# Value products in groups of four key blocks, the transposed maxima three half key blocks later, and three feature chunks around the change of token halves

## Chip, cores and metric

The kernel runs on one core of a Trainium2 chip. The metric is device time in microseconds of one execution, as the median of several runs.

## What is computed

A decoder block over 2048 tokens of width 1024. One input projection of the normalised tokens feeds two branches. Branch A is latent attention with 8 heads, dense and causal. Branch B is sparse attention with 8 query heads and 2 key/value heads: an indexer scores every visible key, and each query keeps its 256 best.

```python
rel = jax.nn.relu(jnp.einsum('bqhd,bsd->bqhs', qib, k_idx))     # indexer, 8 heads
score = jnp.einsum('bqhs,bqh->bqs', rel, wb)                    # then causal mask
_, sel = lax.top_k(score, k_top)                                # k_top = 256
...
merged = sigmoid(m_a + b_merge[0]) * (o_a @ w_branch_mla) + sigmoid(m_b + b_merge[1]) * (o_b @ w_branch_dsa)
x = x + merged @ w_out
```

`o_a` and `o_b` are the softmax attentions of the two branches, each times the SiLU of its own gate projection.

## The kernel before

The work goes in four stages. **Tokens** (0 to about 344 us of the span): normalise, transpose, project queries, keys and index inputs. The transposed tokens are kept as a high and a low part, `hT0h`, `hT0l`, `hT1h`, `hT1l`, each 128 partitions by 8 by 512 floats (2 MiB), and only 1024 of the 2048 tokens fit; the first half goes to DRAM as `d_h` while the second half is projected.

**Features** (344 to about 1083 us): 96 feature chunks, 24 column groups (gates and merge gates) by 4 groups of 512 tokens. `FEATURES` is their order: first the token half that is on the chip, column group by column group, on `hT0` and then `hT1`; then the other half, which `load_h(g)` brings back from `d_h` into the same two tile pairs as soon as the last chunk that reads them is through. Around that change of halves the order takes two column groups on `hT0` and then the same two on `hT1`, so that a reload has two chunks of time. `load_w` and `load_split` bring the weights of a column group into three buffers `wf`. Each chunk is 24 matmuls in four slots. Between the slots, three lanes are advanced at fixed rates: `index_pair` (the indexer's scores of two query tiles into a tile `sc`, two buffers), `search` (a threshold search on the scores of the pair before: five rounds of a ScalarE Sign pass over each of the two tiles, then mask, removal and bias; 1.3 of its pieces a slot), and `prepare` (queries and keys of branch A).

**Attention** (1058 to 1967 us): `pipeline` runs 32 units (branch, group of 512 queries, pair of heads), of 4, 8, 12 or 16 key blocks. A key block is, for each of two heads, the scores `st` (L646, for branch B with eight small mask products more), Exp on ScalarE into `pt` (L674) and the row sums `acc` (L684, one head on GpSimd, one on VectorE). The value products `o` (L690) are held back: `flush` lets them go in groups of two key blocks, by the first half of a later key block. They use 64 columns of the array for each head, all the other products here use 128. Between the halves `fill` takes pieces of the coming units at an even rate: each piece is one product `ap` (L600) whose row maximum VectorE reads (L604 or L607); then a piece with the last reductions and `nm` (L614); then the piece that transposes the 8 columns of maxima on TensorE (L623), copies them (L625) and sends them by DMA into a row of the coming unit's query tile. `LEAD` is how many half key blocks ahead of the unit's start the pieces are to be through. `finish` multiplies `o` by the gates `og` (L700), stores it, and for every second unit sums the `acc` tiles over the partitions (L708).

**Merge** (1967 to 2339 us): branch projections, merge, output projection.

TensorE's order is the order in which the program is written. The order on the other engines and on the DMA queue is set by a planner at build time, which takes what is ready in its own model of time and prefers what is written earlier.

Of the kernel before, what the change touches and what calls it, by code (L numbers as in the profile page):

```python
# [20 lines left out]
P = 128  # L21
# [19 lines left out]
PREPARE_GAP = 17  # L41
SEARCH_RATE = 1.3
PRIORITY = 200
SEARCH_GAP = 4
INDEX_FIRST = 7
HEADS_FIRST = 10
TAIL = 3
WAIT = 0
LEAD = 6
PT_BUFS = 10  # L50
WINDOW = 8.5
EVALS = 5
PAIRS = [(NT - 1 - n, 2 + n) for n in range(7)]
# [18 lines left out]
class Block:  # L72
# [133 lines left out]
    def hidden(self, tok, t):  # L206
        nc = self.nc
        x = tok.tile([P, D], F32, name="x", tag="x", bufs=X_BUFS)
        nc.sync.dma_start(x, self.a["x"][t * P:(t + 1) * P, :])
        if t == 0:  # L210
            nc.sync.dma_start(self.gnorm, bcast(self.a["norm_gain"], D))
        junk = tok.tile([P, D], BF, name="xj", tag="xj")
        ssq = tok.tile([P, 1], F32, name="xs", tag="xs", bufs=2)
        nc.scalar.activation(junk, x, AF.Square, accum_out=ssq)
        rstd = self.rsqrt(tok, ssq, 1, 1.0 / D, "x")
        nc.vector.scalar_tensor_tensor(x, x, rstd, self.gnorm, op0=OP.mult, op1=OP.mult)
        yield
        i, sl = t % 8, slice(t % 4 * P, t % 4 * P + P)
        hi, lo = (m[:, :, sl] for m in self.hT[i // 4])
        for b in range(2):  # L220
            ps = self.pp.tile([P, 4, P], F32, name="tr", tag="tr", bufs=3)
            for k in range(4):
                kc = 4 * b + k
                nc.tensor.transpose(ps[:, k], x[:, kc * P:(kc + 1) * P], self.ident)
            self.split(nc.scalar, hi[:, 4 * b:4 * b + 4], lo[:, 4 * b:4 * b + 4], ps, eng_lo=nc.vector)
        if t < 8:
            for s, m in enumerate((hi, lo)):
                self.move(self.d_h[t][:, s], m)

    def load_w(self, pool, src, n, name, bufs, engines, stage=None):  # L230
        nc = self.nc
# [101 lines left out]


    def load_h(self, g):
        for i in range(4):
            for s in range(2):
                self.move(self.hT[g][s][:, :, i * P:(i + 1) * P], self.d_h[4 * g + i][:, s])

    def feat(self, ev, hf, g, c, w):  # L340
        nc = self.nc
# [63 lines left out]
    def search(self, ip, n, ts, scs):  # L405
# [27 lines left out]
        for e in range(EVALS):  # L433
# [3 lines left out]
            for i, sc in enumerate(scs):  # L437
                W = sc.shape[1]
                nc.scalar.activation(junk(W), sc, AF.Sign, bias=nt[:, i], accum_out=sg[:, i])  # L439
            v.scalar_tensor_tensor(d, sg, 0.5, guess[:, :, 1:2], op0=OP.mult, op1=OP.add)  # L440
            ma = ip.tile([P, 2, 2, 1], I32, name="ma", tag="ma", bufs=2)
            v.tensor_scalar(ma[:, :, 0], d, 0.0, None, op0=OP.is_gt)
# [14 lines left out]
        for i, (t, sc) in enumerate(zip(ts, scs)):  # L457
# [6 lines left out]
            for r in range(2):  # L464
                v8 = ip.tile([P, 8], F32, name="v8", tag="v8", bufs=2)
                pen = ip.tile([P, 8], F32, name="pen", tag="pen", bufs=2)
                need = ip.tile([P, 1], F32, name="need", tag="need", bufs=2)
                v.max(v8, sc)
                v.tensor_scalar(need, th[:, i, 1:2], -1.0, float(TOPK - 8 * r), op0=OP.mult, op1=OP.add)
                v.tensor_scalar(pen, self.iota8, need, 3.0e38, op0=OP.is_ge, op1=OP.mult)  # L470
                v.tensor_tensor(v8, v8, pen, op=OP.add)
                yield
                v.match_replace(sc, v8, sc, SELECTED)
                yield
            bias = ip.tile([P, S], BF, name="bias", tag="bias", bufs=1)[:, :W]
            nc.scalar.activation(bias, sc, AF.Relu, bias=self.shift)
# [216 lines left out]
    def finish(self, u):  # L693
        nc, at = self.nc, self.at
        b, p, g = u["branch"], u["p"], u["g"]
        while any(s[0] is a for s in self.sums for a in u["acc"]):
            self.add_up()
        og = at.tile([P, 512], F32, name="og", tag="og", bufs=2)
        nc.sync.dma_start(og, self.d_f[4 * b + p][g])
        nc.vector.tensor_tensor(og, u["o"], og, op=OP.mult)  # L700
        nc.sync.dma_start(self.d_o[b][g][:, p], og)
# [25 lines left out]
    def pipeline(self, units, ahead):  # L727
        count = len(units)
        heads, spec, left = [None] * count, [None] * count, [0] * count
        begun, born, clock = 0, [0] * count, [0]  # L730

        def begin(n):
            nonlocal begun
            while begun < count and begun - ahead[begun] <= n:
                m = begun
                heads[m] = units[m]()
                spec[m] = next(heads[m])
                left[m] = 8 * (spec[m]["g"] + 1) + 2
                born[m] = clock[0]
                begun += 1  # L740

        def take(n):
            left[n] -= 1
            next(heads[n])

        begin(-1)
# [5 lines left out]

        def flush(keep=1):
            nonlocal after
            if keep and len(values) < 3:
                return
            while len(values) > keep:
                f, u, j = values.pop(0)
# [8 lines left out]
        for n in range(count):  # L767
# [3 lines left out]
            for j in range(u["nk"]):  # L771

                def fill(half):
                    slots, pieces, rate = 2 * (u["nk"] - j) - half - LEAD, 0, 0.0
                    for m in range(n + 1, begun):
                        pieces += left[m]
                        rate = max(rate, pieces / max(slots, 1))
                        slots += 2 * spec[m]["nk"]
                    credit[0] += rate
                    for m in range(n + 1, begun):  # L780
                        while left[m] and credit[0] >= 1.0 and clock[0] >= born[m] + WAIT:
                            take(m)
                            credit[0] -= 1.0

                clock[0] += 1
                values.append((self.scores_t(u, j, fill, flush), u, j))
            after.append((AGE, self.finish, u))
            while n + 1 < count and left[n + 1]:
# [172 lines left out]
    def run(self):  # L961
        nc, a = self.nc, self.a
        self.setup()
        self.d_h = [self.dram([P, 2, KC, P], F32, "d_h%d" % t) for t in range(NT // 2)]
        self.d_qi = [self.dram([P, H, 32], F32, "d_qi%d" % t) for t in range(NT)]
        self.d_c = [self.dram([P, 2, 3, P], F32, "d_c%d" % t) for t in range(NT)]
        self.d_qb = [self.dram([P, H, P], F32, "d_qb%d" % t) for t in range(NT)]
# [244 lines left out]
def feature_order():  # L1212
    order = []
    for half in range(2):
        pairs = [(c,) for c in range(24)]
        pairs = pairs[:22] + [(22, 23)] if half == 0 else [(0, 1)] + pairs[2:]
        order += [(half, g, 24 * half + c) for p in pairs for g in range(2) for c in p]
    return order

# [72 lines left out]
```

## Time and profile before

| | |
|---|---|
| runs | median 2342.23 us (2340.57 to 2347.39, 3 runs) |
| profiled execution | 2340.68 us, span 2338.9 us |
| TensorE matmuls | 2250.8 us busy (96%) |
| VectorE, GpSimd, ScalarE | 1417.3 (61%), 1193.1 (51%), 986.6 us (42%) |
| granted TensorE clock, mean | 0.987 |
| DMA | 326.12 MB, mean 139 GB/s |
| chain that ended last | TensorE 76%, VectorE 9%, GpSimd 6% |

Busy time of TensorE counts each matmul with its modelled end, so consecutive matmuls overlap, and a gap shows only where the pipeline ran empty. The span runs from the first to the last instruction; the time of the execution has 1.8 us around it.

### The profile page before, as it was taken

Reading aid. Unit: us, or ns where it says so; the run is one execution under the profiler, and the core shown is the slowest. Engines: PE = TensorE matmul, PEld = TensorE weight load, DVE = VectorE, ACT = ScalarE, POOL = GpSimd, SP = SyncE. Lnnn points to the kernel's source line nnn. Section 1 sums busy time; section 2 is a strip of 40 time slices with the busy share of each in tenths; the row PEclk is TensorE's granted clock in tenths of the full one; section 3 lists DMA queues with packets and bytes.
Section 4 is the critical chain, followed back from the end, with each engine's and each line's share of the span. In section 5 each row is a group of like instructions: output and inputs, shape, how many; then the busy total and the mean of one; then the engine's idle time right before and its main releaser. Section 6 shows DMA issues by size and latency. Waiting matters only on the chain.

```text
span 2338.9 us, 37920 instructions
## 1 busy us (share of the span) xinstructions
PE 2250.8 (96%) x12882; PEld 1745.5 (75%) x12882; DVE 1417.3 (61%) x3296; ACT 986.6 (42%) x1986; POOL 1193.1 (51%) x1541
## 2 busy tenths in 40 slices
PE   6999999999988999999999999999999999899999
PEld 6999988877776887886555655655655557899988
DVE  6453525588785877856676676677778874322221
ACT  5342325667666677642334434434433443101110
POOL 5875968866754434312344434434774546634432
PEclk9999999999999999999999999999999999999999
DMA  9441345666668655568433322212222102544442
GB/s 311 139 147 54 120 157 166 227 216 196 223 204 262 206 174 180 182 204 240 135 114 102 117 74 64 65 47 71 79 84 82 51 10 78 172 136 141 138 131 77
DMA packets 298100, 326.12 MB, mean 139 GB/s; under 512 B 23408, under 2 KB 228592, under 8 KB 297776
## 3 DMA queue, kind: packets, MB, share of 16 engines
q1 hardware_dynamic: 297392, 323.56, 44.0%
q8 instruction: 101, 1.65, 0.3%
q14 instruction: 95, 0.78, 0.1%
q10 hardware_dynamic: 512, 0.13, 0.0%
HBM read 184.20 MB, written 139.26 MB: 138 GB/s over the span
## 4 chain that ended last, share of the span: by engine, by line
PE 76%; DVE 9%; POOL 6%; issue 3%; ACT 3%; DMA 2%; SPq 0%; DVEq 0%; ACTq 0%; POOLq 0%
PE st L646 18%; PE o L690 11%; PE acc L113 8%; PE acc L115 8%; PE acc L114 8%; PE ap L600 5%; PE ou L115 2%; PE ou L114 2%; PE ou L113 2%; PE br L114 2%; PE br L113 2%; PE br L115 2%; DVE sc L392 2%; PE z L387 2%; ACT junk L439 1%
## 5 line engine op out<-in xcount | busy, mean ns | idle before, releaser
L674 ACT ACTIVATE pt<-st 128x512 f32<-128x512 f32 (+3 forms) x640 | 340.1, 534 | 466.7 <-PE st L646 417.1
L684 POOL TENSOR_TENSOR acc<-acc,pt 128x512 f32<-128x512 f32 (+3 forms) x288 | 328.2, 1140 | 347.8 <-ACT pt L674 337.9
L392 DVE SCALAR_TENSOR_TENSOR sc<-zr,w_i,sc 128x512 f32<-128x512 f32 (+3 forms) x266 | 214.8, 810 | 111.0 <-ACT zr L389 106.9
L646 PE MATMUL st<-Q,K 96*128 96x512 f32 (+3 forms) x960 | 265.8, 384 | 0.6 <-issue 0.6
L604 DVE TENSOR_REDUCE mx<-ap 128x1 f32<-128x512 f32 (+2 forms) x320 | 185.1, 604 | 110.3 <-PE ap L600 63.6
L684 DVE TENSOR_TENSOR acc<-acc,pt 128x512 f32<-128x512 f32 (+3 forms) x288 | 223.4, 776 | 46.5 <-ACT pt L674 43.1
L607 DVE CUSTOM_DVE_ANT_0 mj<-ap,mask 128x512 bf16<-128x512 f32 (+2 forms) x320 | 193.5, 605 | 91.1 <-PE ap L600 81.9
L646 PEld LDWEIGHTS st<-Q,K 96*128 96x128 f32 (+1 forms) x960 | 163.4, 192 | 73.7 <-issue 50.9
L389 ACT ACTIVATE zr<-z 128x512 f32<-128x512 f32 (+3 forms) x304 | 163.0, 545 | 97.1 <-PE z L387 91.5
L113 PE MATMUL acc<-hT1h,wfh 128*128 128x512 f32 x384 | 156.9, 409 | 9.4 <-DMA hT1h<-d_h 7.0
L113 PE MATMUL acc<-hT0h,wfh 128*128 128x512 f32 x384 | 155.2, 404 | 0.7 <-DMA hT0h<-d_h 0.7
L114 PE MATMUL acc<-hT1l,wfh 128*128 128x512 f32 x384 | 151.9, 396 | 1.6 <-DMA d_f<-ev 1.6
L115 PE MATMUL acc<-hT1h,wfl 128*128 128x512 f32 x384 | 152.5, 397 | 0.0
L114 PE MATMUL acc<-hT0l,wfh 128*128 128x512 f32 x384 | 150.9, 393 | 1.1 <-DMA hT0l<-d_h 1.1
L115 PE MATMUL acc<-hT0h,wfl 128*128 128x512 f32 x384 | 151.6, 395 | 0.0
L690 PE MATMUL o<-pt,Vb 128*64 128x512 f32 (+3 forms) x640 | 138.7, 555 | 0.0
L690 PE MATMUL o<-pt,V 128*64 128x512 f32 (+3 forms) x640 | 136.2, 547 | 0.0
L646 PE MATMUL st<-Q,Kd 128*128 128x512 f32 (+3 forms) x320 | 132.9, 416 | 0.0
L106 ACT ACTIVATE mh<-sg 128x256 fp32r<-128x256 f32 x64 | 26.7, 417 | 231.3 <-POOL sg L931 231.2
L929 DVE TENSOR_TENSOR sg<-br,sg 128x256 f32<-128x256 f32 x128 | 53.7, 424 | 115.7 <-PE br L115 102.6
L387 PE MATMUL z<-kT,iqT 128*128 128x512 f32 (+3 forms) x304 | 111.5, 371 | 11.1 <-ACT zr L389 11.1
L646 PE MATMUL st<-Q,Kl 65*128 65x512 f32 (+3 forms) x320 | 117.3, 367 | 0.0
(283 smaller groups left out, 5923.3 us busy)
## 6 DMA issues: line engine op xcount, KB each, us to landing
d_f<-ev SPq DMA_DIRECT2D x96, 256.0 KB
sg<-d_f SPq DMA_DIRECT2D x128, 128.0 KB
wst<-in_w_f SPq DMA_DIRECT2D x96, 128.0 KB
d_w<-wfh SPq DMA_DIRECT2D x24, 512.0 KB
d_w<-wfl SPq DMA_DIRECT2D x24, 512.0 KB
d_q<-phl SPq DMA_DIRECT2D x32, 384.0 KB
d_k<-phl SPq DMA_DIRECT2D x32, 384.0 KB
wfh<-d_w SPq DMA_DIRECT2D x24, 512.0 KB
```

What stands on the lines that cost most here:

```text
L113: mm(ps, lhi, rhi, start=start, stop=False)
L114: mm(ps, lhi, rlo, start=False, stop=False)
L115: mm(ps, llo, rhi, start=False, stop=stop)
L387: nc.tensor.matmul(z[:, :n], qT[:, h], self.kT[:, k0:k0 + n], start=True, stop=True)
L389: nc.scalar.activation(r[:, :n], z[:, :n], AF.Relu)
L392: nc.vector.scalar_tensor_tensor(sc[:, k0:k0 + n], r[:, :n], ws, sc[:, k0:k0 + n], op0=OP.mult, op1=OP.add)
L604: nc.vector.tensor_reduce(mx[:, b:b + 1], ps[:, :n], axis=AX, op=OP.max)
L607: nc.vector.tensor_tensor_reduce(out=junk[:, :n], in0=ps[:, :n], in1=mask[i][:, 512 * b:512 * b + n], scale=1.0, scalar=-3.0e38, op0=OP.su ...
L646: nc.tensor.matmul(banks[hh][:, cols], l, r, start=start and n == 0, stop=stop and n == len(seq) - 1)
L674: nc.scalar.activation(pt[:, n0:], ps[:, n0:], AF.Exp, scale=u["scale"])
L684: eng.tensor_tensor(acc[:, n0:], acc[:, n0:], pt[:, n0:], op=OP.add)
L690: self.nc.tensor.matmul(u["o"][64 * hh:64 * hh + 64, n0:], u["v"](hh, j), pts[hh][:, n0:], start=(j == 0), stop=(j == u["nk"] - 1))
```

## The change

- `GROUP = 4`: value products go in groups of four key blocks; `pt` has 12 buffers for 10, `og` one for two.
- `SETTLE = 3`: the last piece of a unit's maxima, the transposition, is taken only when three half key blocks have passed since the piece before it. `LEAD` is 7 for 6. `WAIT` was 0 and held nothing back.
- The search has a piece boundary behind each Sign pass, one more wait in each of the five rounds, and three more pieces between the last removal and the bias pass of each tile: 53 pieces for 32.
- Around the change of halves the order takes three column groups on `hT0`, then the same three on `hT1`. `d_h` is one DRAM tile for each 512 tokens, and `load_h` fetches it by pairs of the 8 planes, in the order in which the matmuls read them: pieces of 4096 bytes, where it was 512.

```diff
--- before.py
+++ after.py
@@ -41,13 +41,14 @@
 PREPARE_GAP = 17
 SEARCH_RATE = 1.3
 PRIORITY = 200
-SEARCH_GAP = 4
+SEARCH_GAP = 5
 INDEX_FIRST = 7
 HEADS_FIRST = 10
 TAIL = 3
-WAIT = 0
-LEAD = 6
-PT_BUFS = 10
+LEAD = 7
+SETTLE = 3
+PT_BUFS = 12
+GROUP = 4
 WINDOW = 8.5
 EVALS = 5
 PAIRS = [(NT - 1 - n, 2 + n) for n in range(7)]
@@ -225,7 +226,7 @@
             self.split(nc.scalar, hi[:, 4 * b:4 * b + 4], lo[:, 4 * b:4 * b + 4], ps, eng_lo=nc.vector)
         if t < 8:
             for s, m in enumerate((hi, lo)):
-                self.move(self.d_h[t][:, s], m)
+                self.move(self.d_h[t // 4][:, s, :, sl], m)
 
     def load_w(self, pool, src, n, name, bufs, engines, stage=None):
         nc = self.nc
@@ -333,9 +334,9 @@
 
 
     def load_h(self, g):
-        for i in range(4):
+        for k in range(0, KC, 2):
             for s in range(2):
-                self.move(self.hT[g][s][:, :, i * P:(i + 1) * P], self.d_h[4 * g + i][:, s])
+                self.move(self.hT[g][s][:, k:k + 2], self.d_h[g][:, s, k:k + 2])
 
     def feat(self, ev, hf, g, c, w):
         nc = self.nc
@@ -437,6 +438,7 @@
             for i, sc in enumerate(scs):
                 W = sc.shape[1]
                 nc.scalar.activation(junk(W), sc, AF.Sign, bias=nt[:, i], accum_out=sg[:, i])
+                yield
             v.scalar_tensor_tensor(d, sg, 0.5, guess[:, :, 1:2], op0=OP.mult, op1=OP.add)
             ma = ip.tile([P, 2, 2, 1], I32, name="ma", tag="ma", bufs=2)
             v.tensor_scalar(ma[:, :, 0], d, 0.0, None, op0=OP.is_gt)
@@ -471,6 +473,8 @@
                 v.tensor_tensor(v8, v8, pen, op=OP.add)
                 yield
                 v.match_replace(sc, v8, sc, SELECTED)
+                yield
+            for _ in range(3):
                 yield
             bias = ip.tile([P, S], BF, name="bias", tag="bias", bufs=1)[:, :W]
             nc.scalar.activation(bias, sc, AF.Relu, bias=self.shift)
@@ -695,7 +699,7 @@
         b, p, g = u["branch"], u["p"], u["g"]
         while any(s[0] is a for s in self.sums for a in u["acc"]):
             self.add_up()
-        og = at.tile([P, 512], F32, name="og", tag="og", bufs=2)
+        og = at.tile([P, 512], F32, name="og", tag="og", bufs=1)
         nc.sync.dma_start(og, self.d_f[4 * b + p][g])
         nc.vector.tensor_tensor(og, u["o"], og, op=OP.mult)
         nc.sync.dma_start(self.d_o[b][g][:, p], og)
@@ -727,7 +731,8 @@
     def pipeline(self, units, ahead):
         count = len(units)
         heads, spec, left = [None] * count, [None] * count, [0] * count
-        begun, born, clock = 0, [0] * count, [0]
+        begun = 0
+        turn, taken = [0], [0] * count
 
         def begin(n):
             nonlocal begun
@@ -736,11 +741,11 @@
                 heads[m] = units[m]()
                 spec[m] = next(heads[m])
                 left[m] = 8 * (spec[m]["g"] + 1) + 2
-                born[m] = clock[0]
                 begun += 1
 
         def take(n):
             left[n] -= 1
+            taken[n] = turn[0]
             next(heads[n])
 
         begin(-1)
@@ -752,7 +757,7 @@
 
         def flush(keep=1):
             nonlocal after
-            if keep and len(values) < 3:
+            if keep and len(values) <= GROUP:
                 return
             while len(values) > keep:
                 f, u, j = values.pop(0)
@@ -777,12 +782,12 @@
                         rate = max(rate, pieces / max(slots, 1))
                         slots += 2 * spec[m]["nk"]
                     credit[0] += rate
+                    turn[0] += 1
                     for m in range(n + 1, begun):
-                        while left[m] and credit[0] >= 1.0 and clock[0] >= born[m] + WAIT:
+                        while left[m] and credit[0] >= 1.0 and (left[m] > 1 or turn[0] >= taken[m] + SETTLE):
                             take(m)
                             credit[0] -= 1.0
 
-                clock[0] += 1
                 values.append((self.scores_t(u, j, fill, flush), u, j))
             after.append((AGE, self.finish, u))
             while n + 1 < count and left[n + 1]:
@@ -961,7 +966,7 @@
     def run(self):
         nc, a = self.nc, self.a
         self.setup()
-        self.d_h = [self.dram([P, 2, KC, P], F32, "d_h%d" % t) for t in range(NT // 2)]
+        self.d_h = [self.dram([P, 2, KC, 512], F32, "d_h%d" % g) for g in range(2)]
         self.d_qi = [self.dram([P, H, 32], F32, "d_qi%d" % t) for t in range(NT)]
         self.d_c = [self.dram([P, 2, 3, P], F32, "d_c%d" % t) for t in range(NT)]
         self.d_qb = [self.dram([P, H, P], F32, "d_qb%d" % t) for t in range(NT)]
@@ -1213,7 +1218,7 @@
     order = []
     for half in range(2):
         pairs = [(c,) for c in range(24)]
-        pairs = pairs[:22] + [(22, 23)] if half == 0 else [(0, 1)] + pairs[2:]
+        pairs = pairs[:21] + [(21, 22, 23)] if half == 0 else [(0, 1, 2)] + pairs[3:]
         order += [(half, g, 24 * half + c) for p in pairs for g in range(2) for c in p]
     return order
 
```

## Rows read from the trace of the kernel before

**Rows 1.** Windows of attention: us, busy (instructions) of PE PEld DVE ACT POOL, clock, DMA.

```profile
1090.00:1967.00 877.00, 858.40 (x4951) 517.44 (x4949) 625.66 (x1681) 354.12 (x682) 417.47 (x395) 0.99 0.27 79
...
1540.00:1760.00 220.00, 213.75 (x1247) 130.46 (x1247) 170.49 (x467) 87.34 (x167) 123.33 (x116) 0.98 0.23 71
```

**Rows 2.** Waits of TensorE: for whom, us in total, times, longest.

```profile
PE ap L623 <- DVE nm L614: 16.4, 17, 2.2
...
PE z L387 <- ACT zr L389: 11.1, 6, 3.3
...
PE acc L113 <- DMA hT1h<-d_h: 7.0, 1, 7.0
...
PE ap L600 <- DVE mx L607: 1.0, 2, 0.8
```

**Rows 3.** TensorE in time order, a group of value products, branch A: start, us.

```profile
1640.65 0.40 PE L600 MATMUL ap<-Kd,Q 128*128 128x512 f32 x1
1640.89 0.40 PE L646 MATMUL st<-Q,K 97*128 97x512 f32 x1
1641.22 0.65 PE L690 MATMUL o<-pt,V 128*64 128x512 f32 x2
1641.70 1.46 PE L690 MATMUL o<-pt,V 128*64 128x512 f32 x6
1642.13 1.03 PE L690 MATMUL o<-pt,V 128*64 128x512 f32 x4
1643.09 0.73 PE L646 MATMUL st<-Q,K 96*128 96x512 f32 x2
1643.65 0.40 PE L600 MATMUL ap<-Kd,Q 128*128 128x512 f32 x1
```

**Rows 4.** The same in branch B, without and with value products behind the masks.

```profile
1943.60 0.62 PE L646 MATMUL st<-negb,mask 128*128 128x128 bf16 x8
1944.03 0.48 PE L646 MATMUL st<-Q,Kd 128*128 128x512 f32 x1
...
1945.05 0.62 PE L646 MATMUL st<-negb,mask 128*128 128x128 bf16 x8
1945.60 0.65 PE L690 MATMUL o<-pt,Vb 128*64 128x512 f32 x2
```

**Rows 5.** Windows at half clock, TensorE alone: us, busy (instructions), granted clock.

```profile
743.55:753.79 10.24, 4.37 (x10) 0.50 0.98 307
1108.78:1115.60 6.82, 6.58 (x17) 0.50 0.51 146
...
1747.07:1750.48 3.41, 3.41 (x15) 0.50 0.03 6
...
518.28:521.69 3.41, 3.41 (x11) 0.50 0.97 295
```

**Rows 6.** DMA rate from 724 to 748 us, in 40 slices of 0.6 us.

```profile
GB/s 411 389 375 389 416 399 403 404 372 416 430 410 423 409 345 316 334 335 335 337 300 309 298 261 258 275 278 252 306 306 288 317 310 227 255 271 199 234 266 306
DMA packets 9739, 7.90 MB, mean 329 GB/s; under 512 B 285, under 2 KB 8463, under 8 KB 9738
```

**Rows 7.** One transposition of maxima and the VectorE work ahead of it.

```profile
1570.55 1.23 DVE L684 TENSOR_TENSOR acc<-acc,pt 128x512 f32<-128x512 f32 x1
...
1572.08 0.27 PE L623 MATMUL ap<-ident,nm 128*8 128x128 f32 x1 [2.20 <-DVE nm L614]
```

**Rows 8.** Groups by line and shape on VectorE: count, busy us, mean ns, idle before.

```profile
L684 DVE TENSOR_TENSOR acc<-acc,pt 128x512 f32<-128x512 f32 x192 | 177.7, 926 | 27.4 <-ACT pt L674 24.6 <-POOL acc L682 2.1
...
L607 DVE CUSTOM_DVE_ANT_0 mj<-ap,mask 128x512 bf16<-128x512 f32 x224 | 153.3, 684 | 62.0 <-PE ap L600 57.7 <-DVE nm L614 0.4
```

**Rows 9.** ScalarE around the end of the first search.

```profile
515.53 2.00 ACT L476 ACTIVATE bias<-sc,shift 128x2048 bf16<-128x2048 f32 x1 [4.98 <-DVE sc L473]
...
521.97 0.60 ACT L378 ACTIVATE iqT<-tr 128x512 fp32r<-128x512 f32 x1 [1.91 <-PE tr L118]
523.30 0.62 ACT L476 ACTIVATE bias<-sc,shift 128x384 bf16<-128x384 f32 x1 [0.74 <-DMA d_m<-bias]
```

## Prediction

> **What bounds the kernel now.** I read the page first: TensorE is 96% busy and makes up 76% of the chain that ended last, so only what shortens TensorE's own sequence can shorten the run. Then the windows by stage: in attention TensorE is busy 858.40 of 877 us, VectorE 625.66; in the most loaded quarter VectorE reaches 170.49 of 220 us, 77% [rows 1]. No engine stands close behind TensorE there, but VectorE is the next. Then the waits of TensorE: two kinds carry names that the diff touches, the transposition of the maxima (16.4 us in 17 waits) and the reload of the token halves (7.0 us in one), and a third, the indexer's products waiting for ScalarE (11.1 us), lies beside the search [rows 2]. Busy time hides a fourth loss: the timeline shows TensorE slow while it is busy, at each change between value products and the others [rows 3, 4], and in stretches in which the clock granted is the lower of its two levels, 1.2 for 2.4 GHz [rows 5].
>
> **Groups of four.** Two products of 512 columns start 0.24 us apart. Around a group in branch A I read: last product before it to the group 0.33 us (0.09 more); first pair of passes to the second 0.48 where the next takes 0.43 (0.05); the last pair to the next product: 0.96 from the third pair's start, less 0.43, is 0.53 (0.10); the first two products behind the group 0.56 where two take 0.48 (0.08). Together 0.32 us a group [rows 3]. In branch B the group stands behind eight mask products; these take 0.43 us up to the next product without a group and 0.55 up to the group (0.12); with the same 0.05 and 0.10 that is 0.27, the product behind being slow in both cases [rows 4].
> How many groups: the units have 320 key blocks (in each branch 16 units of 4, 8, 12 or 16). Counting through `flush`, it lets two go at every second block, 159 times, and now four at every fourth, 79 times: 80 fewer. 40 are in branch B and 16 of branch A's stand behind a diagonal mask product, as in B: 56 at 0.27 and 24 at 0.32 us are 15.1 + 7.7 = 23 us. Bounds: 18 (0.22 each, if a change costs less among four) and 26 (0.32 each).
> The products themselves stay as many. What the longer holding needs: five key blocks of `pt` are alive, ten of twelve buffers. A unit's `finish` comes up to two groups of four behind its end, where it was two groups of two; `o` has one buffer, but its next writer is now four key blocks away instead of two. One `og` costs nothing: load, multiply and store come once a unit, 877 us over 32 units or 27 us apart on average. In seven places a short unit lets the third `acc` buffer wait for L708 within the same key block; GpSimd stands there for at most one block, 877/320 = 2.7 us, and six blocks of `pt` cover it.
>
> **Transposition three half blocks later.** The row shows the cause: VectorE does a 1.23 us addition ahead of the last reductions, and TensorE stands 2.20 us at L623 [rows 7]. Counting through `fill`, the 30 transpositions now come 1 to 3 half blocks behind the last row-maximum product, and 3 to 5 afterwards. Two more half blocks are 2.7 us (877/640 each 1.37), more than the longest wait of 2.2. So the 16.4 us go, and with them the half clock: four of these waits (1109, 1397, 1572 and 1747 us) are followed by half-clock stretches of 6.82 and three times 3.41 us [rows 5], 17.1 us, in which half is lost: 8.5. Prize 24.9; I take 22, since a few waits will outlast two half blocks. Bounds: 12 and 25. The other end of that piece is the unit's start: its copy and its DMA must land before the unit's first product. By the same count it comes 5 half blocks ahead once and otherwise at least 6, where it was at least 7. Six are 8.2 us for a copy and a small DMA; TensorE's waits have no line for that row today [rows 2], and no piece is forced to the end of a unit in the count. I put it at nothing, and at 1 us for each of 30 units if the cover is gone.
>
> **Change of halves.** 2 x 2 MiB have to come between the last chunk of one order and the first of the next. A chunk takes (1083 - 344)/96 = 7.7 us, so the time goes from 15.4 to 23.1 us. In the window from 723 us on the DMA engines move 7.90 MB at 329 GB/s, and TensorE waits 7.0 us [rows 2, 6], then runs 4.37 us at half clock [rows 5], 2.2 lost. The first 9 us of that window, in which the weights `wf` come in rows of 4096 bytes, run near 400 GB/s, the rest, with the 512-byte pieces, at 200 to 340 [rows 6]. At 329 GB/s 4.2 MB are 12.8 us, with one weight pair ahead of them (1.05 MB) and as much of other traffic 19 us: it fits into 23. Gain: 7.0 + 2.2 and shorter waits of the same kind on both halves, which I put at 2: 11 us; bounds 8 and 14. The cost is that three weight buffers are held through six chunks, so that a weight pair has two chunks, 15 us, to arrive; 1.05 MB take 3.2 us at the same rate, and GpSimd has the split to do only in the first half.
> The rows and a page differ here. The Trainium skill, "DMA: Bandwidth & Descriptors", section Specifications, has 512 B as the least transfer for line rate; by that, longer pieces would bring no faster reload, and the gain would rest on the third chunk alone, some 10 us for 11. The trace does not agree: the 4096-byte rows beside them were faster by a quarter.
>
> **Search.** TensorE waits 11.1 us on the indexer's relus [rows 2], the longest of it at 518 us, and behind that it runs 3.41 us at half clock [rows 5]. The cause is seen on ScalarE: the bias pass stands first in its queue and waits 4.98 us for VectorE's last removal, and the relus wait behind it [rows 9]. Three more pieces ahead of the bias pass and a boundary between the Sign passes let relus go first. I take 7 of about 14 us. Bounds: the whole 14, or a loss of 8, since the first search ends at 523.3 us, 1.3 us after the next pair but one has begun with its transposes at 521.97, and that pair needs its `sc` buffer.
>
> **What comes back.** With groups of four, TensorE issues row-maximum products in denser runs. Of a key block of 2.7 us its values take (1643.09 - 1641.22)/2 = 0.94 [rows 3], which leaves 1.8. VectorE wants two maxima at 0.684 and one addition at 0.926 for it, 2.3 us [rows 8]. Four blocks in a row put it 2.0 us behind, two blocks 1.0. Four `ap` buffers hold about four half blocks, 3.6 us, and TensorE waits for them 1.0 us today [rows 2]. I take 4 us; bounds 0 and 24 (0.3 us for each of 79 groups).
>
> **Sum.** 23 + 22 + 11 + 7 - 4 = 59 us. The profiled execution took 2340.7 us, 1.5 below the median of the runs: 2281.7, and 2283 as a median.
>
> **Rivals.**
> *VectorE takes the groups' gain back.* Against it 77% load in the fullest quarter, for it the static order of each queue. Without the 23 us and with the 4 already counted: 2306.
> *The wait of the transposition only moves* to the next `ap` product or to the unit's first score, because the reductions stay as late. Against it: only 1.0 us of waits on `ap` today, and no work of VectorE is added. Without the 22: 2305.
> *The reload gets slower.* `d_h` rows lie 32 KiB apart for 8 KiB. At the slowest slice of the window, 199 GB/s [rows 6], 6.3 MB take 32 us, 9 more than the three chunks have, at each of the halves: 18 lost and none of the 11 gained, 2312. The Trainium skill has such a rule, in "DMA: Bandwidth & Descriptors", Latency and other measured facts: copies slow down at large power-of-two row pitches; its smallest is 512 KiB, and no row here shows this layout.
> *Slower: the search becomes the pace.* If its pieces set its length, 21 more at 1.3 a slot of 1.92 us (7.7/4) make it 31 us longer. The first ended at 523.3 us [rows 9], just as its buffer was wanted; it would then hold up the third pair by some 30 us, the fourth by perhaps 15, two more by 5 to 10, and its last end would hold up the first query and key tiles, which take its room, by up to 25: 80 us lost for 7 gained, 2370. It decides from about 66 us of such holds. Against it: the search is late by its chain of ScalarE and VectorE steps, not by its pieces, and the planner holds nothing back that is ready.
>
> **Chances.** The forecast 0.70, with its own range 2266 to 2298; VectorE 0.09; the moved wait 0.06; the reload 0.03; the search 0.05, the only one that is slower; better than all my middle values (search and clock in full) 0.04; and several of the small losses together, ending near the old time, 0.03. 0.3% of 2342 is 7 us, about what a measurement of this kernel tells from no change. Faster 0.92, same 0.03, slower 0.05. The range 2262 to 2308 leaves out the search, the reload, the small losses together, the best case and the forecast's own edges, 0.18.
>
> **What would show it.** Groups: pairs of value passes still 0.43 us apart, and 79 groups where there were 159. Transposition: L623's waits below 3 us and no half clock behind it. Reload: no wait of `acc` for `hT1h`, and no stretch of 10 us at half clock near 745 us. Search: relu waits below 5 us and the bias pass without its wait. VectorE: waits of `ap` on L604 and L607 below 5 us. The forecast is wrong if these waits come up elsewhere: `ap` on VectorE, `st` on a query tile's row, `z` on the search.

## The result, and the profile after

| | before | after |
|---|---|---|
| runs | 2342.72 us (2340.57 to 2347.39, 4 runs) | 2317.36 us (2310.96 to 2326.29, 4 runs) |
| ratio of times | | 0.9888, interval 0.986 to 0.9916 |
| profiled execution: span | 2338.9 us | 2309.2 us |
| TensorE busy, mean granted clock | 2250.8 us, 0.987 | 2223.1 us, 0.992 |

The kernel became faster by some 25 us; 59 were forecast, and the time lies above the range. The profiled execution is the fastest of the four (2310.96 us), 30 below that of before. The mean granted clock of the four falls from 0.992 in the fastest to 0.985 in the slowest (2326.29 us). In the changed kernel the lines of features stand one lower (the relus: L388 and L390), those of attention four: row maxima L604, L608 and L611, last reductions L617 and L618, transposition L627, scores L650, Exp L678, sums L688, values L694.

The stages, from the times of their first products in the two traces (us; attention begins with the first row-maximum product; the half clock is the sum of the stretches with a granted clock of 0.50):

| stretch | before | after | gained |
|---|---|---|---|
| start to the 49th feature chunk | 723.1 | 722.7 | 0.5 |
| the next 12 chunks, with the change of halves | 104.5 | 93.6 | 10.9 |
| from there to attention | 231.0 | 231.2 | -0.2 |
| attention | 908.9 | 889.1 | 19.8 |
| merge | 371.4 | 372.7 | -1.3 |
| half clock within attention | 17.1 | 6.8 | |

So the change of halves gave its 11 us, the search gave nothing, and attention gave 20 of the 41 that its terms came to. The two stretches at half clock that are left in attention (window, us, TensorE busy, granted clock, DMA share, GB/s):

```profile
1692.50:1695.90 3.40, 3.22 (x14) 0.50 0.52 149
1890.40:1893.80 3.40, 3.40 (x13) 0.50 0.01 1
```

Ahead of the first TensorE had stood 1.67 us at a row-maximum product, ahead of the second 1.86 us at the transposition. The waits of TensorE after, over the whole span (for whom, us in total, times, longest), beside those of [rows 2]:

```profile
PE ap L627 <- DVE nm L618: 15.7, 12, 1.9
...
PE z L388 <- ACT zr L390: 11.4, 6, 3.3
...
PE ap L604 <- DVE mx L611: 4.2, 6, 1.7
...
PE st L650 <- ACT pt L678: 3.2, 2, 1.6
```

The wait for `hT1h` is gone. The transposition, held back three half key blocks, waits 15.7 us where it was 16.4: in 12 places instead of 17, and nearly as long. The wait for the relus is the one of before. Two that were small have grown: row-maximum products waited 1.0 us [rows 2], and the scores this:

```profile
PE st L646 <- ACT pt L674: 1.1, 1, 1.1
```

The groups themselves do what was counted. TensorE in time order, one group of four in branch A after (start, us):

```profile
1255.85 0.39 PE L650 MATMUL st<-Q,K 97*128 97x512 f32 x1
1256.17 3.65 PE L694 MATMUL o<-pt,V 128*64 128x512 f32 x16
1259.75 0.73 PE L650 MATMUL st<-Q,K 96*128 96x512 f32 x2
1260.33 0.27 PE L627 MATMUL ap<-ident,nm 128*8 128x128 f32 x1
```

Sixteen products take 3.58 us up to the next one. In [rows 3] eight take 1.87 (1641.22 to 1643.09), twice 3.74. That is 0.16 less, and one entry (0.09) and one slow pair behind (0.56 to 0.58 for 0.48, 0.08 to 0.10) go too: 0.33 to 0.35 us for each group saved, where 0.32 was taken.

One transposition after, answering to [rows 7]; TensorE first, then VectorE, in time order (in brackets the idle time before and what ended it):

```profile
1367.33 0.40 PE L604 MATMUL ap<-K,Q 96*128 96x512 f32 x1
...
1369.61 0.34 PE L650 MATMUL st<-Q,Kd 128*128 128x384 f32 x1
1369.79 0.34 PE L650 MATMUL st<-Q,Kl 65*128 65x384 f32 x1
1371.73 0.27 PE L627 MATMUL ap<-ident,nm 128*8 128x128 f32 x1 [1.59 <-DVE nm L618]
```

```profile
1368.48 0.67 DVE L608 TENSOR_REDUCE mx<-ap 128x1 f32<-128x512 f32 x1
1369.08 0.67 DVE L688 TENSOR_TENSOR acc<-acc,pt 128x512 f32<-128x512 f32 x1
1369.67 0.68 DVE L608 TENSOR_REDUCE mx<-ap 128x1 f32<-128x512 f32 x1
1370.27 0.14 DVE L617 TENSOR_REDUCE mx<-mx 128x1 f32<-128x3 f32 x1
1370.34 0.67 DVE L608 TENSOR_REDUCE mx<-ap 128x1 f32<-128x512 f32 x1
1370.93 0.67 DVE L688 TENSOR_TENSOR acc<-acc,pt 128x512 f32<-128x512 f32 x1
1371.53 0.14 DVE L618 TENSOR_SCALAR nm<-mx 128x1 f32<-128x1 f32 x1
```

The reader is to see both sides of a race. TensorE comes from the unit's last maximum product (1367.33) to its transposition in 2.8 us, through three half key blocks with no value product among them, and stands there for 1.59 us. VectorE starts on that product's maximum 1.15 us after the product's start, and puts two additions and two maxima of the next unit ahead of the last reduction, which ends 4.3 us behind the start of the product. The other eleven waits look alike: between the last product and the transposition VectorE does two or three additions and three to six maxima, and is idle for 0.4 us at most.

The change of halves: the DMA rate from 724 to 748 us after, in 40 slices of 0.6 us, answering to [rows 6]:

```profile
GB/s 417 405 409 402 422 413 413 406 410 434 423 430 396 410 403 410 410 389 406 423 420 411 415 403 399 398 403 384 311 205 273 297 21 0 0 0 0 0 0 0
DMA packets 3142, 7.54 MB, mean 314 GB/s; under 512 B 312, under 2 KB 952, under 8 KB 3141
```

About 400 GB/s up to 741 us and through by 744, in a third of the packets. And ScalarE at the end of the first search, answering to [rows 9]:

```profile
510.53 0.60 ACT L390 ACTIVATE zr<-z 128x512 f32<-128x512 f32 x1 [0.86 <-PE z L388]
516.13 2.00 ACT L480 ACTIVATE bias<-sc,shift 128x2048 bf16<-128x2048 f32 x1 [5.00 <-DVE sc L475]
518.04 1.55 ACT L390 ACTIVATE zr<-z 128x512 f32<-128x512 f32 x3
```

The bias pass still stands ahead of three relus and waits 5.00 us, as it waited 4.98.

### The profile page after: what moved, and what is told of

Same layout as the page of the kernel before. It is cut to its first block, busy times and chain, and to the rows that moved or that the text cites. A ratio compares the mean times of both kernels' runs of the same rounds, so it can differ in the third digit from the quotient of the medians.

```text
span 2309.2 us, 37988 instructions
## 1 busy us (share of the span) xinstructions
PE 2223.1 (96%) x12882; PEld 1747.9 (76%) x12882; DVE 1407.8 (61%) x3296; ACT 982.6 (43%) x1986; POOL 1195.3 (52%) x1541
## 4 chain that ended last, share of the span: by engine, by line
PE 72%; DVE 10%; POOL 8%; issue 4%; ACT 3%; DMA 2%; SPq 0%; ACTq 0%; POOLq 0%; DVEq 0%
PE st L650 15%; PE o L694 10%; PE acc L114 8%; PE acc L116 7%; PE acc L115 7%; PE ap L604 5%; PE ou L116 2%; PE ou L115 2%; PE ou L114 2%; PE br L115 2%; PE br L116 2%; PE br L114 2%; DVE sc L393 2%; PE z L388 2%; ACT junk L440 1%
## 5 line engine op out<-in xcount | busy, mean ns | idle before, releaser
L688 POOL TENSOR_TENSOR acc<-acc,pt 128x512 f32<-128x512 f32 (+3 forms) x288 | 331.9, 1153 | 359.7 <-ACT pt L678 350.8
L678 ACT ACTIVATE pt<-st 128x512 f32<-128x512 f32 (+3 forms) x640 | 338.2, 533 | 422.0 <-PE st L650 378.0
L688 DVE TENSOR_TENSOR acc<-acc,pt 128x512 f32<-128x512 f32 (+3 forms) x288 | 232.3, 807 | 44.1 <-ACT pt L678 42.3
L650 PE MATMUL st<-Q,K 96*128 96x512 f32 (+3 forms) x960 | 257.3, 380 | 0.6 <-issue 0.6
L611 DVE CUSTOM_DVE_ANT_0 mj<-ap,mask 128x512 bf16<-128x512 f32 (+2 forms) x320 | 193.2, 604 | 82.0 <-PE ap L604 73.5
L608 DVE TENSOR_REDUCE mx<-ap 128x1 f32<-128x512 f32 (+2 forms) x320 | 183.2, 602 | 74.7 <-PE ap L604 35.7
L390 ACT ACTIVATE zr<-z 128x512 f32<-128x512 f32 (+3 forms) x304 | 162.5, 544 | 90.7 <-PE z L388 87.6
L650 PEld LDWEIGHTS st<-Q,K 96*128 96x128 f32 (+1 forms) x960 | 164.8, 191 | 47.1 <-issue 24.9
L650 PE MATMUL st<-Q,Kd 128*128 128x512 f32 (+3 forms) x320 | 133.4, 417 | 0.0
L694 PE MATMUL o<-pt,Vb 128*64 128x512 f32 (+3 forms) x640 | 127.0, 539 | 0.0
L694 PE MATMUL o<-pt,V 128*64 128x512 f32 (+3 forms) x640 | 125.7, 535 | 0.0
L388 PE MATMUL z<-kT,iqT 128*128 128x512 f32 (+3 forms) x304 | 111.3, 370 | 11.5 <-ACT zr L390 11.4
L604 PE MATMUL ap<-Kd,Q 128*128 128x512 f32 (+2 forms) x320 | 116.3, 378 | 4.4 <-DVE mx L611 4.2
```

Of the source, the lines that this page charges most:

```text
L390: nc.scalar.activation(r[:, :n], z[:, :n], AF.Relu)
L604: nc.tensor.matmul(ps[:, :n], q[:, i * P:(i + 1) * P], k(b)[:, :n], start=True, stop=not diag)
L608: nc.vector.tensor_reduce(mx[:, b:b + 1], ps[:, :n], axis=AX, op=OP.max)
L611: nc.vector.tensor_tensor_reduce(out=junk[:, :n], in0=ps[:, :n], in1=mask[i][:, 512 * b:512 * b + n], scale=1.0, scalar=-3.0e38, op0=OP.su ...
L650: nc.tensor.matmul(banks[hh][:, cols], l, r, start=start and n == 0, stop=stop and n == len(seq) - 1)
L678: nc.scalar.activation(pt[:, n0:], ps[:, n0:], AF.Exp, scale=u["scale"])
```

## The experiments

In each, attention is given by the trace (before 908.9, after 889.1 us), beside the median of the runs and its ratio to the kernel before on the same chip, with its 95% interval.

How far such a reading can be trusted, three of these kernels show, which leave attention as it is in the changed kernel: the last reductions preferred, the search in 32 pieces, and two column groups. VectorE's instructions there come in the same order, and the transposition waits 15.6 or 15.7 us in 12 places, yet attention took 895.8, 892.7 and 892.4 us where it was 889.1, with 20.5, 17.1 and 17.1 us at half clock where it was 6.8. With half of those stretches taken off, the four are 883.8 to 885.7 us. So some us between two traces can be the clock alone, and the time at half clock is given with each.

### Parts of the change alone, and undone

**Groups of two** in the changed kernel:

```diff
-GROUP = 4
+GROUP = 2
```

> The changed kernel with groups of two key blocks again (79 groups become 159), all else kept. Both theories: 23 us are lost with the groups. Dense runs (between groups of four TensorE outruns VectorE, so the maxima come late and three half key blocks are too short): with groups of two the waits of L627 fall from 15.7 to below 6 us and no half clock follows them, so the time is about 2317 + 23 - 13 = 2327 us. Queue order (the planner puts the last reductions behind other VectorE work whatever the groups): L627 still waits 13 to 18 us, and the time is about 2340 us.

Measured: 2310.37 us, 0.9849 (0.9836 to 0.9862); attention 884.5 us, and no half clock in it. Without the groups of four attention is 4.6 us shorter than in the trace with them, and as long as the four traces above without their half clock: what the groups save goes into waits, and the half clock behind them comes on top. Both theories had counted 23 us as lost with the groups; none of it was. The waits of TensorE in attention:

```profile
PE st L650 <- ACT pt L678: 1.6, 1, 1.6
PE ap L604 <- DVE mx L608: 1.4, 1, 1.4
PE ap L627 <- DVE nm L618: 1.0, 2, 0.5
```

So holding the transposition back does remove its wait, if the groups are of two.

**The transposition not held back**, in groups of four:

```diff
-SETTLE = 3
+SETTLE = 0
```

> The changed kernel with SETTLE = 0: groups of four, the transposition at once again. Dense runs: L627 waits over 25 us, more than in the kernel before (16.4), with four or more half-clock stretches; about 2317 + 15 = 2332 us. Queue order: the wait is set by where the reductions stand, so it grows by at most 5 us; about 2320 us.

Measured: 2343.72 us, 0.9991 (0.998 to 1.0002), slower than both theories had it; attention 919.5 us. The transposition waits 34.9 us in 26 places, and 34.1 us run at half clock: the groups of four double the wait that was to be removed.

**The groups of four alone**, in the kernel before, with their buffers:

```diff
-PT_BUFS = 10
+PT_BUFS = 12
...
-        og = at.tile([P, 512], F32, name="og", tag="og", bufs=2)
+        og = at.tile([P, 512], F32, name="og", tag="og", bufs=1)
...
-            if keep and len(values) < 3:
+            if keep and len(values) <= 4:
```

> The kernel before with groups of four alone (12 pt buffers, one og). The gain of the groups by themselves is 23 us. Dense runs: the waits of the transposition (L623) grow from 16.4 to over 25 us and those of ap to 5 us, about 2342 - 23 + 13 = 2332 us. Queue order: they stay at 16 to 20 us, about 2320 us.

Measured: 2367.43 us, 1.0087 (1.0072 to 1.0101), slower; attention 933.8 us with 58.0 us at half clock, in a trace of the slowest of its six runs (2373.53 us), and over the whole span:

```profile
PE ap L623 <- DVE nm L614: 43.4, 23, 2.9
```

27.0 us more of this wait than in [rows 2] and half of 40.9 us more at half clock are 47.5 us lost, and attention is 24.9 longer: the groups save some 22 us by this count, and in this run give back twice that. The median lies 35 us above the slower of the two expectations.

**The transposition alone**, in the kernel before:

```diff
-WAIT = 0
-LEAD = 6
+LEAD = 7
+SETTLE = 3
...
-                        while left[m] and credit[0] >= 1.0 and clock[0] >= born[m] + WAIT:
+                        while left[m] and credit[0] >= 1.0 and (left[m] > 1 or turn[0] >= taken[m] + SETTLE):
```

> The kernel before with the transposition held back three half blocks, and nothing else of the change. Theory: in groups of two this part gives what it was forecast to give, attention 884 to 887 us (908.9), and the reload of the token halves stays as it was: 2316 to 2322 us. Rival: the gain of the changed kernel in groups of two came from the other parts (search, buffers, reload): attention above 895 us, 2328 us or more.

Measured: 2324.21 us, 0.9908 (0.989 to 0.9927), 22.6 below the kernel before on the same chip (2346.85); attention 886.5 us, with 1.2 us of waits at the transposition and no half clock. Where the groups stay as they were, the term of 22 us comes out as 22.4 in attention. The 12 chunks around the change of halves take 104.8 us, as before.

**The search in 32 pieces** again:

```diff
-SEARCH_GAP = 5
+SEARCH_GAP = 4
...
-                yield
...
-            for _ in range(3):
-                yield
```

> The changed kernel with the search's pieces as before (32 for 53). If the new pieces neither help nor cost, as the relu waits of 11.4 us for 11.1 suggest: the same time, 2315 to 2319 us. If they took a cost away that the profile does not name: 2322 us or more. If they delay something: 2312 us or less.

Measured: 2315.01 us, 0.9873 (0.9852 to 0.9894), and 11.6 us of waits on the relus; attention 892.7 us, 17.1 of it at half clock. The search's part gave nothing and cost nothing that these runs tell apart.

**Two column groups around the change of halves**, with the new pieces of the reload kept:

```diff
-        pairs = pairs[:21] + [(21, 22, 23)] if half == 0 else [(0, 1, 2)] + pairs[3:]
+        pairs = pairs[:22] + [(22, 23)] if half == 0 else [(0, 1)] + pairs[2:]
```

> The changed kernel with two column groups around the change of halves again; the reload by pairs of planes in 4096-byte pieces is kept. If the third chunk is what removed the wait: hT1 waits 5 us or more again with half clock behind it, 2326 us. If the longer pieces and their order did it: no wait over 1 us, the same 2317 us.

Measured: 2320.84 us, 0.99 (0.9882 to 0.9917); attention 892.4 us, 17.1 of it at half clock. No wait for `hT`, and the 12 chunks take 93.6 us: the whole gain of the reload comes from its pieces and their order, not from the third chunk.

### What the waits hang on

**The last reductions preferred** by the planner:

```diff
+            with self.tc.high_priority(offset=PRIORITY):
+                if nb > 1:
+                    nc.vector.tensor_reduce(mx[:, 0:1], mx[:, 0:nb], axis=AX, op=OP.max)
+                nc.vector.tensor_scalar(nm[:, i:i + 1], mx[:, 0:1], -1.0, None, op0=OP.mult)
```

> The changed kernel with the two last reductions of each query block's maxima (L617, L618) preferred by the planner over other VectorE work. Queue order: L627's waits fall below 5 us with the half clock behind them gone, about 2317 - 14 = 2303 us. Dense runs: only the part behind the last row maximum goes, some 1 us for each of 12 waits; L627 still waits about 8 us, about 2311 us.

Measured: 2315.42 us, 0.9869 (0.9853 to 0.9885); attention 895.8 us. VectorE's whole order came out as it was, so this tells nothing of what another order would give; the transposition waits 15.7 us in 12 places as in the changed kernel, and 20.5 us of attention ran at half clock for 6.8 there.

**Held back six half blocks:**

```diff
-LEAD = 7
-SETTLE = 3
+LEAD = 10
+SETTLE = 6
```

> The changed kernel with SETTLE = 6 and LEAD = 10: groups of four, but six half key blocks between the last reductions and the transposition, so that by count 23 of 30 transpositions have a group of value products ahead of them (7 with SETTLE = 3). Dense runs: L627's waits fall from 15.7 to below 4 us and the groups' 23 us come out; attention some 18 us shorter than in the changed kernel, about 2317 - 21 = 2296 us. Rival, that groups of four are dear by themselves: the waits go, but attention is no shorter than the 884.5 us of groups of two, 2308 us or more.

Measured: 2309.97 us, 0.9853 (0.9832 to 0.9875); attention 886.2 us, 13.7 of it at half clock. The wait of the transposition is gone, and this came in its place:

```profile
PE ap L604 <- DVE mx L611: 8.3, 13, 2.6
PE st L650 <- ACT pt L678: 5.0, 4, 2.3
PE st L650 <- DMA Q<-nmT: 1.0, 2, 0.8
```

All waits of TensorE in attention together are 16.3 us where they were 24.0: more distance cures the place and leaves two thirds of the wait.

**VectorE without the sign change**: the last reduction writes `nm` itself, and ScalarE's copy of the transposed maxima changes the sign, 256 VectorE instructions of 0.147 us fewer.

```diff
-            mx = hd.tile([P, 4], F32, name="mx", tag="mx", bufs=4)
+            mx = hd.tile([P, 4], F32, name="mx", tag="mx", bufs=4) if nb > 1 else nm[:, i:i + 1]
...
-                nc.vector.tensor_reduce(mx[:, 0:1], mx[:, 0:nb], axis=AX, op=OP.max)
-            nc.vector.tensor_scalar(nm[:, i:i + 1], mx[:, 0:1], -1.0, None, op0=OP.mult)
+                nc.vector.tensor_reduce(nm[:, i:i + 1], mx[:, 0:nb], axis=AX, op=OP.max)
...
-        nc.scalar.activation(nmT, ps[0:8, 0:P], AF.Copy)
+        nc.scalar.activation(nmT, ps[0:8, 0:P], AF.Copy, scale=-1.0)
```

> The changed kernel without the sign change on VectorE (L618, 256 instructions of 0.15 us; the copy behind the transposition takes the sign): one step fewer behind the last maximum, 37 us less for VectorE, groups of four kept. Dense runs: VectorE is still behind, the waits of L627 fall from 15.7 to some 8 to 11 us, about 2308 us. Queue order: the last step that other work overtakes is gone, waits below 4 us, about 2299 us.

Measured: 2302.89 us, 0.982 (0.9802 to 0.9839), the fastest kernel of this study that leaves nothing out; attention 879.2 us, 13.7 of it at half clock. Its waits in attention:

```profile
PE ap L604 <- DVE mx L611: 5.3, 6, 2.6
PE ap L626 <- DVE nm L617: 4.8, 7, 1.7
```

All waits in attention fall from 24.0 to 13.5 us. Whether the shorter chain or the 37 us less of VectorE's work does it was not told apart.

**The same in groups of two:**

```diff
-GROUP = 4
+GROUP = 2
```

> The changed kernel without VectorE's sign change, in groups of two. Theory: in groups of two nothing waits for VectorE any more (1.0 us at the transposition), so the shorter chain gains little there: attention 881 to 885 us, 2304 to 2310 us, slower than the 2302.9 of groups of four without the sign change. Rival: groups of four are worse by themselves, as with the sign change; then it is 4 us or more below 2302.9.

Measured: 2311.33 us, 0.9862 (0.9847 to 0.9877); attention 885.2 us, 3.4 of it at half clock. With a lighter VectorE groups of four are 6.0 us better in attention, where with the sign change they are 4.6 worse.

**Without the sign change, in groups of four, held back six half blocks:**

```diff
-LEAD = 7
-SETTLE = 3
+LEAD = 10
+SETTLE = 6
```

> The changed kernel without the sign change and with the transposition held back six half blocks. Theory: the 4.8 us of waits at the transposition go and those of the row-maximum products (5.3 us) stay or grow, since VectorE's load comes in the same runs: 2296 to 2304 us. Rival: the wait only moves in full, as it partly did with the sign change in (8.3 us at the row-maximum products, 5.0 for the exponentials): 2302 to 2308 us, no gain.

Measured: 2307.82 us, 0.9841 (0.9827 to 0.9856); attention 881.0 us, 10.2 of it at half clock. The transposition's wait is gone, the row-maximum products wait 6.9 us for `mx` and 1.1 for `nm`, the scores 1.4 for the row of maxima, and all waits together are 13.5 us as without the holding back. The rival holds: the wait only moves.

**VectorE without its additions**, in groups of four and of two. These two leave out the additions of every second head's row sums on VectorE (GpSimd's stay; the first block's copy adds 1), so that those sums lack what is left out.

```diff
-        else:
+        elif eng is not self.nc.vector:
             eng.tensor_tensor(acc[:, n0:], acc[:, n0:], pt[:, n0:], op=OP.add)
```

> The changed kernel without VectorE's additions to the denominators (285 of 0.81 us, 230.6 us in attention); GpSimd's stay, so that the denominators of every second head are too small. Theory: the groups of four save their 18 to 23 us on TensorE, and it is VectorE's order of reductions and additions that gives them back. Then the waits for nm and mx together fall from 20.3 to below 5 us and attention takes 861 to 869 us (889.1 in the changed kernel), some 2285 to 2292 us in all. Rival: the loss comes from elsewhere (the exponentials, the holding of pt, the clock): attention stays above 880 us, some 2303 or more.

> The same without VectorE's additions, in groups of two. Theory: with VectorE out of the way the groups of two take 18 to 23 us longer than the groups of four in attention, 880 to 885 us, as long as they take with the additions (884.5). Rival: groups of four save nothing by themselves, and the two are within 8 us of each other.

Measured: 2286.88 us, 0.9761 (0.9746 to 0.9776) in groups of four, 2306.57 us, 0.9848 (0.9832 to 0.9864) in groups of two; attention 862.2 us, 3.4 of it at half clock, and 882.1 us with none. In groups of two the 230 us of additions cost TensorE next to nothing (884.5 with them); in groups of four they cost 26.9 us. With VectorE out of the way groups of four are worth 19.9 us. What is left of the waits in groups of four:

```profile
PE st L650 <- ACT pt L678: 4.2, 2, 2.7
PE ap L627 <- DVE nm L618: 1.3, 2, 0.6
```

**Two fifths of these additions on GpSimd** instead, with the sign change and without it:

```diff
-nc.vector if hh and j else nc.gpsimd
+nc.vector if hh and j and j // 4 % 2 == 0 else nc.gpsimd
```

> The changed kernel with the additions of key blocks 4 to 7 and 12 to 15 of the second head on GpSimd instead of VectorE, two fifths of those of VectorE. Theory: it is VectorE's load that gives the groups' saving back, so part of the 20.3 us of waits for nm and mx goes: attention 872 to 884 us (889.1), 2298 to 2310 us in all. Rival: two fifths are not enough or GpSimd, now busy some 550 of 889 us at 1.15 us an addition, is late itself, and waits of the value products or of VectorE for the sums take their place: attention 886 us or more, no gain.

> The same without VectorE's sign change. Theory: VectorE has both loads less, attention 868 to 878 us (879.2 without the sign change alone), 2292 to 2302 us. Rival: what was left (4.8 us of waits at the transposition, 5.3 at the row-maximum products) is not VectorE's load, or GpSimd becomes late: 2302.9 or more.

Measured: 2313.34 us, 0.9861 (0.9838 to 0.9884) and 2308.69 us, 0.983 (0.9809 to 0.9851); attention 886.5 and 886.0 us, 13.7 and 23.9 of it at half clock. The expected gain did not come. With the sign change the transposition's wait halves (7.4 us in 7), but row-maximum products wait 7.7 us in 3. The groups of the full-width additions in attention (count, busy us, mean ns, idle before), first the changed kernel, then this one:

```profile
L688 DVE TENSOR_TENSOR acc<-acc,pt 128x512 f32<-128x512 f32 x192 | 184.5, 961 | 15.5 <-ACT pt L678 14.5
```

```profile
L688 DVE TENSOR_TENSOR acc<-acc,pt 128x512 f32<-128x512 f32 x112 | 126.2, 1127 | 30.4 <-POOL acc L688 21.4 <-ACT pt L678 8.4 <-ACT nmT L629 0.3
```

VectorE's remaining additions became slower, 961 to 1127 ns, and it stood 21.4 us for sums that GpSimd had in hand, with the maxima queued behind. The Trainium skill, "Perfetto Trace Analysis", section Optimizing Scalar/DVE Operations, warns that moving work between these two engines might not help, since they share a read port; the trace agrees with the warning, and how much of the missing gain is due to the slower additions, to the hand-over of the sums and to the half clock was not told apart.

## Why the prediction was wrong, step by step

Of the 59 us the profiled execution gained 29.7. Of what is missing, about 20 us are the term for what comes back, 7 the search, and 3 the groups.

**Groups of four, 23 us.** Right, at the lower side: 0.33 to 0.35 us a group in branch A by the rows, 19.9 us between the two kernels without VectorE's additions (bounds 18 to 26), of which the one with groups of four still has 3.4 us more of waits and 3.4 us at half clock. 80 groups in the trace where there were 160.

**Transposition, 22 us.** Right alone (22.4 in attention), and the step that failed once the groups were of four: "Two more half blocks are 2.7 us (877/640 each 1.37)". The mean half block holds its share of the value products, 0.94/2 = 0.47 us [rows 3]; one without them is 1.37 - 0.47 = 0.90, and two are 1.8 us, less than the longest wait of 2.2 that they were to cover. In the order of TensorE's trace 20 of 30 transpositions held back have a value group between the unit's last maximum product and themselves in groups of two, and only 5 of 30 in groups of four (7 were counted before the run of six half blocks). The distance from that product to the transposition as TensorE reaches it (without its wait) is 1.84 us before, 3.31 after and 4.76 in groups of two (medians over the 32 units): in groups of two it grew by 2.9 us, where 2.7 was counted, and in groups of four by 1.5. The two terms were added as if independent, and one takes away the time that the other counts on. Meanwhile VectorE needs longer, from that product to the end of `nm` 2.0 us before, 2.6 after, 2.3 in groups of two. The race that was to be won by 0.5 us (2.7 against 2.2) is lost by up to 1.9.

**What comes back, 4 us.** The mechanism was right (denser row-maximum products put VectorE behind) and the size was not: about 24 us came back, the upper bound. Groups of four should shorten attention by the 19.9 us above and lengthen it by 4.6, in the trace with the least half clock of the four with this attention; in the three others they lengthen it by 8 to 11. The waits in attention account for 19.3 of the 24.5 (23.5 after against 4.2 in groups of two), the 6.8 us of half clock for 3.4. The place was wrong too: it was looked for at the `ap` buffers, which did take 4.6 us, still within the sign that was set for them (below 5), and 15.7 stood where VectorE's chain is read at its end, at the transposition. The working held VectorE's lag of 2.0 us against a cover of four buffers, and never added that lag to the transposition's own chain. The rival that said so, VectorE taking the groups' gain back, 2306 us, was the right one; without the search's 7 us it is 2313. What was held against it, 77% load in the fullest quarter, is the share of an average: in the changed kernel VectorE was idle for 28% of attention (busy 639.32 of 888 us) and late at 12 transpositions.

**Change of halves, 11 us.** 10.9 measured. Of its two reasons one was not needed: with two column groups around the change the gain is the same. The Trainium skill's 512 B in "DMA: Bandwidth & Descriptors", section Specifications, by which the third chunk alone would count, doesn't fit: 512-byte pieces ran at 200 to 340 GB/s [rows 6], 4096-byte ones at about 400. The rival of the slower reload is out by the same rows; its transfers take 4 KiB of each 32 KiB at a time, where the prediction wrote 8.

**Search, 7 us.** Nothing. The prediction read the cause rightly (the bias pass first in ScalarE's queue) and took it that three pieces more ahead of it would let relus go first. The row shows that at this search they do not: it still stands ahead of three relus, with the same wait, and the stretch at half clock at 518 us is there too. Why the bias pass keeps its place behind the added pieces no run shows. The slower rival, the search as the pace, did not come.

**The sum** with what the runs show: 20 + 22 + 11 + 0 - 24 = 29 us, and the profiled execution gained 29.7 in span. The median gained 25; the four runs lie 15 us apart, and the profiled one is the fastest, so that the sum agrees with this execution and is some 4 us more than the median shows.

What is shown is that VectorE's load turns the groups' gain into waits: without its additions groups of four are worth 19.9 us, with them they lose 4.6. What stays open is which of its two loads, additions or maxima, a better order would have to move. No run changed VectorE's order alone, since the planner kept it where the last reductions were preferred. Nor was it tried what is to be had if VectorE's additions did not run beside GpSimd's, where they take longer (see the last section).

## What to carry to other kernels

When two edits stand on the same queue, cost the second in the order that the first leaves: a distance counted in steps is worth only the steps' own content there, not their mean. An engine at three quarters of its time can still be the one that is waited for, if work reaches it in runs; read its lag at the point where its chain is consumed, and look for an instruction in that chain that can go (here a sign change of 0.147 us, done 256 times, worth 9.9 us in attention). And before two traces are compared to a few us, look at how much of each ran at the lower clock.

## What the hardware showed that was not expected

- A VectorE addition of 128 x 512 takes two times. By the changed kernel's trace, 77 of 192 overlap a GpSimd addition for over half of their time and have a median of 1.17 us; the other 115 have 0.69. With two fifths moved to GpSimd the overlapped ones had 1.30.
- The same waits did not bring the same clock: the changed kernel and the one with the last reductions preferred both wait 15.7 us in 12 places at the transposition, longest 1.9, and ran 6.8 and 20.5 us of attention at the lower level of 1.2 GHz.
